# One slot in halves instead of two: the start of an up projection behind a row chain

## The chip, the core and the metric

The kernel runs on one core of a Trainium2 chip. The time is device microseconds of one execution, and the figure that stands for a kernel is the median of its runs. TensorE (PE) does the matmuls and transposes, with weight loads (PEld) that overlap them; VectorE (DVE) and ScalarE (ACT) do the elementwise work and read PE's results from PSUM banks; SyncE (SP) issues the DMAs.

## The reference

One layer of a decoder trunk over 512 positions of 1024 channels: a mixer sub-layer with four branches, then a squared-ReLU MLP, each between two RMS norms and a residual add. Only the seam between the two matters here:

```
mix = merged @ w_out
h   = x + rms_norm(mix, norm_mix_post)
u   = rms_norm(h, norm_mlp_pre)
hid = square(relu(u @ w_up))            # 1024 -> 4096
m   = hid @ w_down                      # 4096 -> 1024
out = h + rms_norm(m, norm_mlp_post)
```

All is float32 in and out.

## The kernel before, in words

Each float32 operand of a matmul is split into a high part (a rounded copy, ACT, L167) and a low part (what is left, DVE, L168), and a product is three matmuls: high by high, low by high, high by low (`mm3`, L237 to L240). Weights come as "units" of 128 x 1024 in the order in which they are used; `unit()` hands out the next one and has those a few ahead loaded (SP) and split.

The 512 positions are four rows of 128 positions, t = 0 to 3 (first to fourth row). Up to the output projection the row is on the partitions: `out_mm(t)` (L867) makes a row's second half of `mix` in a bank `e1[t]`. The first half, `e0`, is made earlier. Then `chain(t)` (L881) runs: ACT squares the bank and sums it, DVE finishes the mean (L847), multiplies by the gain (L884), ACT takes a square root (L855), three small DVE instructions make the reciprocal root (L859 to L861), and two DVE operations over 1024 columns make the residual row `h1` (L886) and the input `u2` of the MLP (L888). The norm before the MLP is not applied with the row's own root here; one known earlier (`rst4`) stands in. The MLP is a squared ReLU between linear maps and is normed again at the end, so the row's own scale only enters through the small constant of that last norm. `row_eps(t)` (L890) works this out from the sum of squares of `h1`: two ACT squares with a read of the sum each, and seven DVE instructions on one element per partition (L845, L847, L893 to L897). Only the end of the kernel reads its result.

The up projection wants `u2` with channels on the partitions. `trans` (L902) turns a row with eight 128 x 128 transposes on PE, and `put` (L911) splits what lies in the bank into `u2h` (ACT) and `u2l` (DVE), 512 columns at a time. Row 0 is turned after `out_mm(2)`, row 1 within `out_mm(3)` (`mid`, L926), rows 2 and 3 within the up projection (L992).

The up projection has 16 slots of 256 hidden channels; a slot takes two units (h = 0, 1) and 48 matmuls of 512 positions (`up_mm`, L945). The first two slots are done in two halves of 256 positions, since rows 2 and 3 come late: first positions 0 to 255 of slots 0 and 1, one unit of each in turn, with the transposes of row 2 behind the second and those of row 3 behind the third; then positions 256 to 511. `up_out` (L958) squares the ReLU of a slot and splits it for the down projection, seven products in place of eight (`form`, `down_group`). The calls of `row_eps` stand behind all this (L1009), and the pools of the mixer are closed ahead of it (L995), so that the down weights' buffers (`load_ab`, L195) reuse the memory of rows that are done with.

The order on each engine is not the program's order but a planner's: it walks a simulated timeline and takes, on each engine, the earliest instruction in program order that it believes ready. `K(...)` holds marked instructions in program order. On the chip each engine then runs its list in that order.

Of the kernel before, what the change touches and what calls it, by code (L numbers as in the profile page):

```python
# [12 lines left out]
AF = mybir.ActivationFunctionType  # L13
ALU = mybir.AluOpType

P = 128
T = 512
D = 1024
NK = D // P
NT = T // P  # L20
# [17 lines left out]
NG = F // (GF * P)  # L38
# [11 lines left out]
def tile_hybrid_trunk(ctx: ExitStack, tc: tile.TileContext, x0, xT, xn, wts, dn, par, bd, cst, msk, gains, out):  # L50
    nc = tc.nc
    act, dve, pool, pe = nc.scalar, nc.vector, nc.gpsimd, nc.tensor
# [17 lines left out]
    K = tc.keep_in_program_order  # L70
# [31 lines left out]
    ident = cp.tile([P, P], F32, name="ident")  # L102
# [6 lines left out]
    rst4 = cp.tile([P, NT], F32, name="rst4")  # L109
# [56 lines left out]
    def split(hi, lo, src, pin=False):  # L166
        a_ = act.activation(hi, src, AF.Copy)  # L167
        d_ = dve.tensor_tensor(lo, src, hi.bitcast(F32), ALU.subtract)  # L168
        if pin:
            K(a_)  # L170
            K(d_)
# [29 lines left out]
    def form(g, n):  # L201
# [22 lines left out]
        split(hi.rearrange("p (j t) -> p j t", j=2), lo.rearrange("p (j t) -> p j t", j=2), src)  # L224
        return hi, lo

    use = [0]
    ahead = [4]
    WARM = 7

    def unit():
        i = use[0]
        use[0] += 1
        prep(i + ahead[0])
        return Wt.hl.pop(i)
# [179 lines left out]
    for c in range(2):  # L415
        for j in range(SCONV):
            src = cx[:, c, PAD - (SCONV - 1) + j : PAD - (SCONV - 1) + j + T]
# [415 lines left out]

    def sq_only(src, t, j):
        dm = s_tile(src.shape[-1])
        act.activation(dm, src, AF.Square, accum_out=stat[:, t, j : j + 1])

    def sq_sum(src, t, j, prev, col):
        sq_only(src, t, j)
# [27 lines left out]
    def out_mm(t, mid=None):  # L867
        e1[t] = sm_bank()
        for k in range(NK):
            if k == 2 and mid:  # L870
                mid()
            wh, wl = wu[k // 2]
            cs = slice((k % 2) * T, (k % 2) * T + T)
            mm3(e1[t], M(0, k, t), M(1, k, t), wh[:, cs], wl[:, cs], k == 0, k == NK - 1)
# [6 lines left out]
    def chain(t):  # L881
        sq = u2[t]
        v = sq_sum(e1[t], t, 1, stat[:, t, 2:3], 3)
        dve.tensor_tensor(sq[:, T:], e1[t], gbc[0][:, T:], ALU.mult)  # L884
        r = row_rstd(v, t)
        dve.scalar_tensor_tensor(h1[t], sq, r, h1[t], ALU.mult, ALU.add)  # L886
        nc.sync.dma_start(h1d[t * P : t * P + P, :], h1[t])
        dve.scalar_tensor_tensor(sq, h1[t], rst4[:, t : t + 1], gbc[1], ALU.mult, ALU.mult)  # L888

    def row_eps(t):  # L890
        e = sq_sum(h1[t][:, :T], t, 4, None, 6)
# [10 lines left out]
    def trans(t, bank):  # L902
        tbs = []
        for j in range(2):
            tb = bank()
            for kk in range(4):
                K(pe.transpose(tb[:, kk * P : kk * P + P], u2[t][:, (4 * j + kk) * P : (4 * j + kk) * P + P], ident))
            tbs.append(tb.rearrange("p (k t) -> p k t", k=4))
        return tbs

    def put(t, j, tv):  # L911
        if u2h[j] is None:
            u2h[j] = up.tile([P, 4, T], F32R, tag="u", name=nm("u2h"))
            u2l[j] = up.tile([P, 4, T], F32R, tag="u", name=nm("u2l"))
        split(u2h[j][:, :, t * P : t * P + P], u2l[j][:, :, t * P : t * P + P], tv)

    for t in range(NT):
        chain0(t)
    for t in range(3):
        out_mm(t)  # L920
        chain(t)
    tb0 = trans(0, sm_bank)
    for j in range(2):
        put(0, j, tb0[j])
# [4 lines left out]
            put(1, j, tb1[j])  # L929

    out_mm(3, mid)
    chain(3)

    mixps.close()
# [4 lines left out]
    def up_bank():  # L939
        return bp.tile([P, 2, T], F32, tag="ub", name=nm("ub"))  # L940

    def dn_bank():
        return dq.tile([P, 2, T], F32, tag="db", name=nm("db"))

    def up_mm(bk, w, h, a, b):  # L945
        wh, wl = w
        for kk in range(4):
            k = 4 * h + kk
            for c in range(2):
                o = kk * W + c * P  # L950
                mm3(bk[:, c, a:b], wh[:, o : o + P], wl[:, o : o + P],
                    U(u2h, k, a, b), U(u2l, k, a, b), k == 0, k == NK - 1)

    HT = T // 2
    NPAIR = 2 * NG
    hid = {}

    def up_out(pair, bk):  # L958
# [19 lines left out]
            split(hi[:, 3:], lo[:, 3:], s)  # L978
        hid[pair] = (hi, lo)

    bks = [up_bank(), up_bank()]
    us = {}
    ahead[0] = 2
    for h in range(2):
        for s in range(2):
            us[s, h] = unit()
            up_mm(bks[s], us[s, h], h, 0, 256)
            if (s, h) in ((1, 0), (0, 1)):
                t = 2 if h == 0 else 3
                tb = dn_bank()  # L990
                for k in range(NK):
                    pe.transpose(tb[:, k // 4, (k % 4) * P : (k % 4) * P + P], u2[t][:, k * P : k * P + P], ident)  # L992
                for j in range(2):
                    put(t, j, tb[:, j].rearrange("p (k t) -> p k t", k=4))
    mix.close()  # L995
    fa = ctx.enter_context(tc.tile_pool(name="fa", bufs=6, reuse_waits="tile"))
    ma = ctx.enter_context(tc.tile_pool(name="ma", bufs=3, reuse_waits="tile"))
# [3 lines left out]
    xp = ctx.enter_context(tc.tile_pool(name="xp", bufs=2, reuse_waits="tile"))  # L1001
    load_ab(0, 0)
    load_ab(0, 1)
    for s in range(2):
        for h in range(2):
            up_mm(bks[s], us[s, h], h, 256, T)
        up_out(s, bks[s])
    ahead[0] = 4
    for t in range(NT):  # L1009
        row_eps(t)  # L1010

    def up_pair(pair):
        bk = up_bank()
# [159 lines left out]
def _layout(inp):  # L1173
    import numpy as np

    a = {k: np.asarray(v) for k, v in inp.items()}
    f4 = np.float32
    x = a["x"][0]
    xt = x.T.reshape(NK, P, T)
    x0 = np.concatenate([xt[0], a["norm_mix_pre"][0].reshape(NK, P).T], axis=1)  # L1180
    xt = xt[1:]
    xn = x.reshape(NT, P, D)

    wi = a["w_in"][0].reshape(2, 4, P, 26, W)
    wb = a["w_branch"][0].reshape(4, 2, P, 2, T)
    wo = a["w_out"][0].reshape(4, 2, P, 2, T)
    wu = a["w_up"][0].reshape(2, 4, P, 16, W)
    wd = a["w_down"][0].reshape(32, P, D)
    units = []

    def slot(w, s):
        for h in range(2):
            units.append(w[h, :, :, s].transpose(1, 0, 2).reshape(P, D))

    for n in SLOT_ORDER:
        if n == "c_g":
            continue
        if n != "c_i":
            slot(wi, SLOT[n])
            continue  # L1200
        for u in range(4):
            w = wi[u // 2, 2 * (u % 2) : 2 * (u % 2) + 2]
            units.append(np.concatenate([w[:, :, SLOT["c_i"]], w[:, :, SLOT["c_g"]]], axis=2).transpose(1, 0, 2).reshape(P, D))
    units[1], units[2] = units[2], units[1]
    for k in GATE_ORDER:
        for dh in range(2):
            for j in range(2):
                slot(wi, 10 + 4 * k + 2 * dh + j)
            units.append(wb[k, :, :, dh].transpose(1, 0, 2).reshape(P, D))
    for eh in range(2):  # L1210
        for ku in range(4):
            units.append(wo[ku, :, :, eh].transpose(1, 0, 2).reshape(P, D))

    def upg(g):
        n = len(units)
        for s in range(2):
            slot(wu, 2 * g + s)
        if g == 0:
            units[n + 1], units[n + 2] = units[n + 2], units[n + 1]

    upg(0)
    for g in range(1, NG):
        upg(g)
    for j in range(GF):
        units.append(wd[GF * (NG - 1) + j])
    wts = np.stack(units)
    dn = wd.reshape(NG, 2, 2, P, D)[: NG - 1].transpose(0, 2, 3, 1, 4)

    def cols(v):
        return v.reshape(-1, 2, P).transpose(2, 0, 1).reshape(P, -1)  # L1230

    win = np.repeat(np.array(WINS), 64)
    pos = np.arange(1, PAD + 1)
    corr = (win[:, None] / np.minimum(pos[None, :], win[:, None])).astype(f4)
    par = np.concatenate([
        cols(a["lru_conv_w"][0]), cols(a["lru_conv_b"]), cols(a["lru_b_a"]), cols(a["lru_b_x"]),
        cols(a["lru_lambda"]), cols(a["pool_scale"]), cols(a["hgrn_lower_bound"]),
        np.concatenate([a["hgrn_norm"][0], a["hgrn_norm"][0]])[:, None],
        cols(a["sconv_w"][0]),
        cols((1.0 / win).astype(f4)),  # L1240
        corr.reshape(2, P, PAD).transpose(1, 0, 2).reshape(P, 2 * PAD),
        (np.arange(P)[:, None] // 64 == np.arange(2)[None, :]).astype(f4),
    ], axis=1)

    def blocks(w):
        n, b = w.shape[0], w.shape[1]
        o = np.zeros((2, P, P), f4)
        for i in range(n):
            c, r = divmod(i * b, P)
            o[c, r : r + b, r : r + b] = w[i]  # L1250
        return o

    bd = np.concatenate([blocks(a["lru_w_a"][0]), blocks(a["lru_w_x"][0]), blocks(a["pool_w"][0])]).transpose(1, 0, 2)
    s = np.arange(P)[:, None]
    msk = []
    for B in MASKED:
        odd = np.arange(P)[(np.arange(P) // B) % 2 == 1][None, :]
        msk.append(s // B == odd // B - 1)
    msk = np.stack(msk).transpose(1, 0, 2).astype(f4)
    cst = np.eye(P, dtype=f4)[None]  # L1260
    gains = np.concatenate([a["norm_mix_post"], a["norm_mlp_pre"], a["norm_mlp_post"]])
    return [x0, xt, xn, wts, dn, par, bd, cst, msk, gains]
# [21 lines left out]
```

## Time and profile before

| what | value |
|---|---|
| median of 3 runs | 745.53 us (745.18 to 745.75) |
| the profiled execution's own time | 745.06 us |
| its span, first to last instruction | 743.3 us |
| PE busy | 735.2 us (99%), 3458 matmuls and transposes |
| DVE busy | 535.8 us (72%) |
| ACT busy | 314.9 us (42%) |
| granted TensorE clock, mean | 0.999 of full speed |

The span leaves out what lies before the first and behind the last instruction. Busy time of a pipelined PE overlaps itself, so PE's pace is read from start to start of its matmuls. A time in a timeline counts from the start of the span.

### The profile page before, as it was taken

Reading aid. Unit: us, or ns where it says so; the run is one execution under the profiler, and the core shown is the slowest. Engines: PE = TensorE matmul, PEld = TensorE weight load, DVE = VectorE, ACT = ScalarE, POOL = GpSimd, SP = SyncE. Lnnn points to the kernel's source line nnn. Section 1 sums busy time; section 2 is a strip of 40 time slices with the busy share of each in tenths; the row PEclk is TensorE's granted clock in tenths of the full one; section 3 lists DMA queues with packets and bytes.
Section 4 is the critical chain, followed back from the end, with each engine's and each line's share of the span. In section 5 each row is a group of like instructions: output and inputs, shape, how many; then the busy total and the mean of one; then the engine's idle time right before and its main releaser. Section 6 shows DMA issues by size and latency. Waiting matters only on the chain.

```text
span 743.3 us, 8800 instructions
## 1 busy us (share of the span) xinstructions
PE 735.2 (99%) x3458; PEld 616.9 (83%) x3458; DVE 535.8 (72%) x784; ACT 314.9 (42%) x411; POOL 6.4 (1%) x11
## 2 busy tenths in 40 slices
PE   9999999999999999999999999999999999999996
PEld 7888888888888888888888988888888888888885
DVE  6798346559997476654748785788769595976797
ACT  7434222336324322232444566544445362635332
POOL 1100000000000000000000000000000000000000
PEclk9999999999999999999999999999999999999999
DMA  9634333222322253323332704142322415030322
GB/s 327 246 115 142 91 106 88 84 86 85 93 82 82 85 216 100 100 94 114 114 113 86 276 37 172 55 142 86 126 101 90 137 57 169 1 114 28 109 91 113
DMA packets 22761, 84.59 MB, mean 114 GB/s; under 512 B 2624, under 2 KB 3520, under 8 KB 20928
## 3 DMA queue, kind: packets, MB, share of 16 engines
q1 hardware_dynamic: 22288, 83.74, 33.5%
q8 instruction: 27, 0.44, 0.3%
q10 hardware_dynamic: 432, 0.29, 0.1%
q14 instruction: 14, 0.11, 0.1%
HBM read 79.83 MB, written 4.19 MB: 113 GB/s over the span
## 4 chain that ended last, share of the span: by engine, by line
PE 98%; DVE 1%; DMA 0%; issue 0%; ACT 0%; DVEq 0%
PE mm L238 14%; PE mm L239 14%; PE mm L240 14%; PE ub L238 8%; PE ub L240 8%; PE ub L239 8%; PE db L238 6%; PE db L240 6%; PE db L239 6%; PE mm L323 3%; PE sm L240 2%; PE sm L239 2%; PE sm L238 2%; PE sm L606 2%; PE tb L1118 0%; PE tb L1117 0%
## 5 line engine op out<-in xcount | busy, mean ns | idle before, releaser
L167 ACT ACTIVATE whi<-raw 128x1024 fp32r<-128x1024 f32 x98 | 103.8, 1062 | 231.0 <-PE mm L239 105.3
L168 DVE TENSOR_TENSOR wlo<-raw,whi 128x1024 fp32r<-128x1024 f32 x98 | 119.5, 1222 | 77.7 <-ACT whi L167 77.5
L240 PE MATMUL mm<-uh,wlo 128*128 128x512 f32 x336 | 131.0, 390 | 0.0
L239 PE MATMUL mm<-ul,whi 128*128 128x512 f32 x336 | 130.9, 389 | 0.0
L238 PE MATMUL mm<-uh,whi 128*128 128x512 f32 x336 | 130.5, 390 | 0.0
L238 PE MATMUL ub<-u2h,whi 128*128 128x512 f32 (+1 forms) x288 | 105.3, 366 | 0.0
L239 PE MATMUL ub<-u2l,whi 128*128 128x512 f32 (+1 forms) x288 | 105.2, 365 | 0.0
L240 PE MATMUL ub<-u2h,wlo 128*128 128x512 f32 (+1 forms) x288 | 105.2, 365 | 0.0
L238 PE MATMUL db<-fhi,ahi 128*128 128x512 f32 x196 | 76.3, 389 | 0.0
L239 PE MATMUL db<-flo,ahi 128*128 128x512 f32 x196 | 76.3, 389 | 0.0
L240 PE MATMUL db<-fhi,alo 128*128 128x512 f32 x196 | 76.2, 389 | 0.0
L240 PEld LDWEIGHTS mm<-uh,wlo 128*128 128x128 f32 x336 | 63.1, 188 | 13.0
L238 PEld LDWEIGHTS mm<-uh,whi 128*128 128x128 f32 x336 | 63.1, 188 | 13.0
L239 PEld LDWEIGHTS mm<-ul,whi 128*128 128x128 f32 x336 | 63.1, 188 | 12.9
L238 PEld LDWEIGHTS ub<-u2h,whi 128*128 128x128 f32 x288 | 54.2, 189 | 8.9 <-DVE u2l L168 0.3
L240 PEld LDWEIGHTS ub<-u2h,wlo 128*128 128x128 f32 x288 | 54.3, 189 | 8.8
L239 PEld LDWEIGHTS ub<-u2l,whi 128*128 128x128 f32 x288 | 54.3, 189 | 8.7
L167 ACT ACTIVATE fhi<-x 128x1024 fp32r<-128x1024 f32 x28 | 29.7, 1061 | 41.1 <-PE db L240 26.5
L1049 DVE TENSOR_TENSOR rows<-rows,db 128x1024 f32<-128x1024 f32 x24 | 29.2, 1218 | 21.8 <-PE db L240 21.7
L238 PEld LDWEIGHTS db<-fhi,ahi 128*128 128x128 f32 x196 | 36.8, 188 | 7.8 <-DVE macc L1049 0.2
L240 PEld LDWEIGHTS db<-fhi,alo 128*128 128x128 f32 x196 | 36.8, 188 | 7.7
L239 PEld LDWEIGHTS db<-flo,ahi 128*128 128x128 f32 x196 | 36.8, 188 | 7.6
(319 smaller groups left out, 1110.6 us busy)
## 6 DMA issues: line engine op xcount, KB each, us to landing
raw<-in_wts_dram SPq DMA_DIRECT2D x102, 512.0 KB, 3.5
ab<-in_dn_dram SPq DMA_DIRECT2D x14, 1024.0 KB, 4.9
t<-in_xn_dram SPq DMA_DIRECT2D x8, 512.0 KB, 7.4
h1d<-t SPq DMA_DIRECT2D x4, 512.0 KB, 2.6
hr<-h1d SPq DMA_DIRECT2D x2, 1024.0 KB, 6.9
xt<-in_xt_dram SPq DMA_DIRECT2D x7, 256.0 KB, 5.0
out_dram<-mg SPq DMA_DIRECT2D x3, 512.0 KB, 2.6
t<-in_gains_dram SPq DMA_DIRECT2D x2, 512.0 KB, 5.8
```

The lines of the kernel that those rows point to most:

```text
L167: a_ = act.activation(hi, src, AF.Copy)
L168: d_ = dve.tensor_tensor(lo, src, hi.bitcast(F32), ALU.subtract)
L238: pe.matmul(ps, lh, rh, start=first, stop=False)
L239: pe.matmul(ps, lh, rl, start=False, stop=False)
L240: pe.matmul(ps, ll, rh, start=False, stop=last)
L323: pe.matmul(fb[s_][c], fw[pair[s_]][wi][:, o_ : o_ + P], U(us_, k), start=first and k == 0, stop=last and k == NK - 1)
L606: pe.matmul(bk[ct][:, cs].rearrange("s (h n b) -> s h n b", h=2, b=B), kk_[:, ct, cs], qo, start=True, stop=True)
L1049: dve.tensor_tensor(macc[p], macc[p], ps, ALU.add)
```

## The change

Slot 0 alone is done in halves, with its two units one behind the other; slot 1 is done over all 512 positions. Rows 2 and 3 are transposed in halves of four, each into a bank of its own, with the split pinned in program order (`half_trans`, new). The last row's two wide DVE operations are done in two halves of 512 columns, and its `h1` is stored behind them. `row_eps` moves: rows 0 and 1 behind the chain of the next row, row 2 ahead of the chain of row 3, row 3 behind the last transposes, with its squares pinned. The up units are laid out in plain order.

```diff
@@ -224,6 +224,7 @@
         split(hi.rearrange("p (j t) -> p j t", j=2), lo.rearrange("p (j t) -> p j t", j=2), src)
         return hi, lo
 
+    HT = T // 2
     use = [0]
     ahead = [4]
     WARM = 7
@@ -833,7 +834,9 @@
 
     def sq_only(src, t, j):
         dm = s_tile(src.shape[-1])
-        act.activation(dm, src, AF.Square, accum_out=stat[:, t, j : j + 1])
+        a_ = act.activation(dm, src, AF.Square, accum_out=stat[:, t, j : j + 1])
+        if t == NT - 1 and j > 3:
+            K(a_)
 
     def sq_sum(src, t, j, prev, col):
         sq_only(src, t, j)
@@ -883,9 +886,11 @@
         v = sq_sum(e1[t], t, 1, stat[:, t, 2:3], 3)
         dve.tensor_tensor(sq[:, T:], e1[t], gbc[0][:, T:], ALU.mult)
         r = row_rstd(v, t)
-        dve.scalar_tensor_tensor(h1[t], sq, r, h1[t], ALU.mult, ALU.add)
+        for a, b in ((0, T), (T, D)) if t == NT - 1 else ((0, D),):
+            hv = h1[t][:, a:b]
+            dve.scalar_tensor_tensor(hv, sq[:, a:b], r, hv, ALU.mult, ALU.add)
+            dve.scalar_tensor_tensor(sq[:, a:b], hv, rst4[:, t : t + 1], gbc[1][:, a:b], ALU.mult, ALU.mult)
         nc.sync.dma_start(h1d[t * P : t * P + P, :], h1[t])
-        dve.scalar_tensor_tensor(sq, h1[t], rst4[:, t : t + 1], gbc[1], ALU.mult, ALU.mult)
 
     def row_eps(t):
         e = sq_sum(h1[t][:, :T], t, 4, None, 6)
@@ -912,13 +917,15 @@
         if u2h[j] is None:
             u2h[j] = up.tile([P, 4, T], F32R, tag="u", name=nm("u2h"))
             u2l[j] = up.tile([P, 4, T], F32R, tag="u", name=nm("u2l"))
-        split(u2h[j][:, :, t * P : t * P + P], u2l[j][:, :, t * P : t * P + P], tv)
+        split(u2h[j][:, :, t * P : t * P + P], u2l[j][:, :, t * P : t * P + P], tv, t > 1)
 
     for t in range(NT):
         chain0(t)
     for t in range(3):
         out_mm(t)
         chain(t)
+        if t:
+            row_eps(t - 1)
     tb0 = trans(0, sm_bank)
     for j in range(2):
         put(0, j, tb0[j])
@@ -929,6 +936,7 @@
             put(1, j, tb1[j])
 
     out_mm(3, mid)
+    row_eps(2)
     chain(3)
 
     mixps.close()
@@ -942,16 +950,15 @@
     def dn_bank():
         return dq.tile([P, 2, T], F32, tag="db", name=nm("db"))
 
-    def up_mm(bk, w, h, a, b):
+    def up_mm(bk, w, h, a, b, ks=(0, 4)):
         wh, wl = w
-        for kk in range(4):
+        for kk in range(*ks):
             k = 4 * h + kk
             for c in range(2):
                 o = kk * W + c * P
                 mm3(bk[:, c, a:b], wh[:, o : o + P], wl[:, o : o + P],
                     U(u2h, k, a, b), U(u2l, k, a, b), k == 0, k == NK - 1)
 
-    HT = T // 2
     NPAIR = 2 * NG
     hid = {}
 
@@ -978,20 +985,25 @@
             split(hi[:, 3:], lo[:, 3:], s)
         hid[pair] = (hi, lo)
 
+    def half_trans(t, j):
+        tb = dn_bank()
+        for kk in range(4):
+            c = (4 * j + kk) * P
+            pe.transpose(tb[:, 0, kk * P : kk * P + P], u2[t][:, c : c + P], ident)
+        put(t, j, tb[:, 0].rearrange("p (k t) -> p k t", k=4))
+
     bks = [up_bank(), up_bank()]
-    us = {}
     ahead[0] = 2
-    for h in range(2):
-        for s in range(2):
-            us[s, h] = unit()
-            up_mm(bks[s], us[s, h], h, 0, 256)
-            if (s, h) in ((1, 0), (0, 1)):
-                t = 2 if h == 0 else 3
-                tb = dn_bank()
-                for k in range(NK):
-                    pe.transpose(tb[:, k // 4, (k % 4) * P : (k % 4) * P + P], u2[t][:, k * P : k * P + P], ident)
-                for j in range(2):
-                    put(t, j, tb[:, j].rearrange("p (k t) -> p k t", k=4))
+    us = [unit()]
+    up_mm(bks[0], us[0], 0, 0, HT)
+    half_trans(2, 0)
+    half_trans(2, 1)
+    us.append(unit())
+    up_mm(bks[0], us[1], 1, 0, HT, (0, 2))
+    half_trans(3, 0)
+    up_mm(bks[0], us[1], 1, 0, HT, (2, 4))
+    half_trans(3, 1)
+    row_eps(3)
     mix.close()
     fa = ctx.enter_context(tc.tile_pool(name="fa", bufs=6, reuse_waits="tile"))
     ma = ctx.enter_context(tc.tile_pool(name="ma", bufs=3, reuse_waits="tile"))
@@ -1001,13 +1013,13 @@
     xp = ctx.enter_context(tc.tile_pool(name="xp", bufs=2, reuse_waits="tile"))
     load_ab(0, 0)
     load_ab(0, 1)
-    for s in range(2):
-        for h in range(2):
-            up_mm(bks[s], us[s, h], h, 256, T)
-        up_out(s, bks[s])
+    for h in range(2):
+        up_mm(bks[0], us[h], h, HT, T)
+    up_out(0, bks[0])
+    for h in range(2):
+        up_mm(bks[1], unit(), h, 0, T)
+    up_out(1, bks[1])
     ahead[0] = 4
-    for t in range(NT):
-        row_eps(t)
 
     def up_pair(pair):
         bk = up_bank()
@@ -1211,16 +1223,8 @@
         for ku in range(4):
             units.append(wo[ku, :, :, eh].transpose(1, 0, 2).reshape(P, D))
 
-    def upg(g):
-        n = len(units)
-        for s in range(2):
-            slot(wu, 2 * g + s)
-        if g == 0:
-            units[n + 1], units[n + 2] = units[n + 2], units[n + 1]
-
-    upg(0)
-    for g in range(1, NG):
-        upg(g)
+    for s in range(2 * NG):
+        slot(wu, s)
     for j in range(GF):
         units.append(wd[GF * (NG - 1) + j])
     wts = np.stack(units)
```

## Rows read from the trace of the kernel before

**Rows 1.** the page: span, PE's busy row, the chain that ended last.
```profile
span 743.3 us, 8800 instructions
PE 735.2 (99%) x3458; PEld 616.9 (83%) x3458; DVE 535.8 (72%) x784; ACT 314.9 (42%) x411; POOL 6.4 (1%) x11
...
PE 98%; DVE 1%; DMA 0%; issue 0%; ACT 0%; DVEq 0%
```
**Rows 2.** waits of PE: who <- for whom: total us, times, longest us.
```profile
PE sm L294 <- DVE spt L561: 1.1, 1, 1.1
```
**Rows 3.** PE by form, 404 to 428.7: xcount, busy us, mean ns, idle.
```profile
L238 PE MATMUL ub<-u2h,whi 128*128 128x256 f32 x64 | 18.2, 287 | 0.0
...
L992 PE MATMUL db<-ident,t 128*128 128x128 f32 x16 | 2.1, 272 | 0.0
```
**Rows 4.** timeline of PE, 428 to 443: start us, duration us, engine, line, operation.
```profile
428.14 0.28 PE L239 MATMUL ub<-u2l,whi 128*128 128x256 f32 x1
...
428.62 0.28 PE L240 MATMUL ub<-u2h,wlo 128*128 128x256 f32 x1
...
439.64 0.39 PE L238 MATMUL db<-fhi,ahi 128*128 128x512 f32 x1
...
442.82 0.39 PE L240 MATMUL db<-fhi,alo 128*128 128x512 f32 x1
```
**Rows 5.** the same timeline around the transposes of the third row.
```profile
409.74 1.04 PE L992 MATMUL db<-ident,t 128*128 128x128 f32 x8
...
410.73 0.28 PE L239 MATMUL ub<-u2l,whi 128*128 128x256 f32 x1
```
**Rows 6.** timeline of PE and PEld where the up projection starts.
```profile
403.60 0.39 PE L240 MATMUL sm<-sp,ylo 128*128 128x512 f32 x1
...
403.88 0.19 PEld L238 LDWEIGHTS ub<-u2h,whi 128*128 128x128 f32 x1 [0.31 <-DVE u2l L168]
```
**Rows 7.** timeline of DVE ahead of that start.
```profile
393.43 0.15 DVE L847 SCALAR_TENSOR_TENSOR stat<-stat 128x1 f32<-128x1 f32 x1
...
394.16 0.15 DVE L859 RECIPROCAL stat<-rt 128x1 f32<-128x1 f32 x1
394.35 0.22 DVE L860 SCALAR_TENSOR_TENSOR nt<-stat,nh 128x1 f32<-128x1 f32 x1
394.60 0.16 DVE L861 SCALAR_TENSOR_TENSOR stat<-nt,stat 128x1 f32<-128x1 f32 x1
394.80 1.28 DVE L886 SCALAR_TENSOR_TENSOR t<-t,stat,t 128x1024 f32<-128x1024 f32 x1
...
397.58 0.16 DVE L847 SCALAR_TENSOR_TENSOR stat<-stat 128x1 f32<-128x1 f32 x1 [0.18 <-ACT s L836]
...
402.54 1.28 DVE L168 TENSOR_TENSOR u2l<-mm,u2h 128x512 fp32r<-128x512 f32 x2
```
**Rows 8.** timeline of DVE in the fourth row's chain.
```profile
406.16 0.16 DVE L893 TENSOR_TENSOR stat<-stat,rst 128x1 f32<-128x1 f32 x1
406.36 0.16 DVE L894 TENSOR_TENSOR stat<-stat,rst 128x1 f32<-128x1 f32 x1
...
410.09 0.15 DVE L895 TENSOR_TENSOR stat<-stat 128x1 f32<-128x1 f32 x1
...
411.07 0.16 DVE L895 TENSOR_TENSOR stat<-stat 128x1 f32<-128x1 f32 x1
```
**Rows 9.** timeline of ACT in the same chain.
```profile
404.61 0.62 ACT L836 ACTIVATE s<-t 128x512 f32<-128x512 f32 x1
...
406.46 0.19 ACT L855 ACTIVATE rt<-stat 128x1 f32<-128x1 f32 x1
...
410.81 0.60 ACT L167 ACTIVATE u2h<-db 128x512 fp32r<-128x512 f32 x1 [0.53 <-PE db L992]
```
**Rows 10.** SP's queue and ACT: loads and first use of down weights.
```profile
411.56 1.28 SPq L198 DMA_DIRECT2D ab<-in_dn_dram  x3
...
420.30 1.06 ACT L167 ACTIVATE fhi<-ab 128x1024 fp32r<-128x1024 f32 x1 [1.90 <-PE ub L239]
```

## The prediction, written before the changed kernel was run

> **What bounds the kernel now.** I read the page first: PE is busy for 735.2 of 743.3 us, and the chain that ended last runs through PE for 98% of the span [rows 1]. The waits of PE name one wait of 1.1 us, among the warming matmuls at the start [rows 2]; what follows PE's last matmul is not touched by the change. So a microsecond is won here only by giving PE less to stream, and any wait that is added ahead of PE is paid in full. Then I read the timelines around 404 us, where the changed code runs: PE, then DVE and ACT, which feed it. PE starts the up projection at 403.88, and its first weight load has stood 0.31 us until a DVE instruction that wrote u2l was done; by its own pitch PE would have been there at 403.60 + 0.23 = 403.83 [rows 6]. The instruction is the last of the four that split the first two rows, the pair from 402.54 to 403.82 [rows 7]. It reads the bank that the first up matmul overwrites. Its slack is nil: PE already lost about 0.05 us to it. That is the reading on which this forecast turns.
>
> **The change part by part.**
>
> *Fewer, longer matmuls.* Before, both first slots are done in 256-column halves: 64 matmuls on each of three lines, 192 in all [rows 3]. After, slot 0 keeps 96 of them, and slot 1 has 48 of 512 columns in place of 96. One of 256 columns takes (428.62 - 428.14) / 4 = 0.120 us from start to start, one of 512 takes (442.82 - 439.64) / 14 = 0.227 us [rows 4]. So PE saves 96 x 0.120 - 48 x 0.227 = 11.52 - 10.88 = 0.64 us, all on the path.
>
> The Trainium skill ("TensorE: Matmul & The Clock Gate", section "Back-to-back issue gap") gives the isolated gap of a matmul at full clock as N/2.4 + 2.5 ns: 109 ns and 216 ns. By it the saving would be an estimated 48 x 2.5 ns = 0.12 us, and the time 0.5 us above what I forecast. The trace does not agree: the shorter one costs 13 ns more than half of the longer, not 2.5, so the rows' figure stands.
>
> *Transposes.* Sixteen before and sixteen after [rows 3]. Before they stand in two groups of eight, after in one of eight and two of four. From the start of eight to the second matmul behind them are 0.99 us, less one matmul's 0.12 is 0.87, or 0.109 each [rows 5]; a charge for joining a group, if it is in there, is at most 0.1 us. I take nothing for the added group, with 0 to 0.1 as bounds.
>
> *Sums of squares.* Each row's sum issues two ACT squares with their reads and seven one-element DVE instructions (L845, L847, L893 to L897). Before, all four rows' run from 404.6 on [rows 9], behind the start of the up projection. After, rows 0 and 1 come in program order ahead of the splits of the first two rows, and row 2 ahead of the fourth row's chain. DVE stands still only 0.18 us between 393 us and 403.8 [rows 7]. So 14 small instructions join a full queue whose last one holds PE. Their price: thirteen such instructions start between 410.09 and 411.07, 0.08 us apart; one that needs the one before it starts 0.20 us later (406.16, 406.36) [rows 8]. Low end: the chain of a row has gaps of 0.19, 0.25 and 0.20 us between its own dependent instructions [rows 7], each holding one more; in two rows that hides 6, and 8 x 0.08 - 0.18 = 0.5 us is left. High end: 4 x 0.07 (taken just under that 0.08) + 10 x 0.20 - 0.18 = 2.1 us. And nothing at all, if the planner sets the splits ahead of the sums. I take 0.7 us, all 14 at the low pitch giving 0.9 and the low end 0.5, since before the planner did mix such instructions with others. The cover is gone here, so all 0.7 us is PE's.
>
> The gain of the same move: before, the fourth row's square root sat on ACT behind other rows' squares from 404.61 until 406.46 [rows 9]. After, at most row 2's two are in its way. The wait that goes is off the path, since before PE had 72 half matmuls (8.6 us) and eight transposes between its start and the fourth row's transposes.
>
> *The fourth row in halves.* Two DVE operations of 1.28 us become four of 512 columns, 0.64 (half) to 0.69 us each (a 512-column DVE subtract, two of them taking 1.28 overlapped) [rows 7]: 0.0 to 0.2 us more on DVE, while the first half is ready one operation earlier. Is it in time? With a start at 404.6, PE needs 24 x 0.12 + 8 x 0.109 + 12 x 0.12 = 5.2 us before the first half of row 3 is transposed: 409.8. DVE has the splits done at 404.5, seven small instructions for row 2 (0.6), the chain from L847 to its first wide operation (394.80 - 393.43 = 1.4 in the second row [rows 7]) and two half operations (1.3): 407.8. Slack 2.0 us, and at the second half (411.6 against 409.1) 2.5 us.
>
> *The splits of rows 2 and 3.* These are now pinned and go through two banks for four groups of transposes, so the third group waits until the first split has read its bank. That split's DVE part follows the fourth row's chain, if DVE keeps program order: 409.1 + 0.7 = 409.8 against 409.8. Then the second pass over slot 0 wants row 3's first split at 412.1: transposes until 410.2, 0.3 until ACT starts and 0.6 of copy [rows 9], 0.7 of subtract: 411.8. Both are about even; I take 0, bounds 0 and 0.8.
>
> *What else moves.* The last store of h1 is issued earlier. Row 3's squares, pinned behind the splits, end about 413.7; the first loads of the down weights, into memory that these rows give up, were issued on SP at 411.56 and may go 2 us later. What they feed starts on ACT at 420.30 [rows 10] and on PE at 439.64 [rows 4]: 19 us of cover. Slot 0 is finished 6 us earlier, slot 1's weights are wanted 10 us later; both ease ACT and DVE. POOL's queue has nothing here. All at nothing.
>
> *Sum.* -0.64 + 0.7 + 0 = +0.06 us on a span of 743.3. The profiled execution's own time is 745.06, 1.76 beside the span, and the median of the runs is 745.53, 0.47 above it. So 745.1 for an execution like the profiled one, 745.6 as a median.
>
> **The rivals.**
>
> *The gain stays (744.9).* The splits go ahead of the sums, or the planner hoists the eight transposes of row 2 (0.87 us) into the wait. For it: out of rows of equal readiness the planner mixed freely on DVE [rows 8]. Against: DVE is full, and the sums come first in program order. 745.53 - 0.64 = 744.9.
>
> *The waits win (747.7, slower).* DVE keeps program order with each dependent instruction 0.20 us apart. The split ends at 403.82 + 2.1 = 405.9, PE loses 2.1 us there; row 2's seven (1.1), the chain (1.4) and four halves (2.8) end at 411.2; the first split of row 2 at 411.9, while PE stands at the third group of transposes from 411.1: 0.8 more. 745.53 - 0.64 + 2.1 + 0.8 = 747.8, less the 0.05 lost already, 747.7. It is slower by over 0.2% once the waits pass 0.64 + 1.49 = 2.1 us. For it: the full queue. Against: the small pitch in [rows 8].
>
> *The halves don't do what they say.* The planner puts the second DVE half behind something else, or the transposes of row 3 late among the matmuls of the second pass. Since nothing waits for row 3 before 409.8, this costs at most the 0.64 again: 745.5, which can't be told from the forecast.
>
> **How the numbers follow.** Forecast (waits of 0.4 to 1.4 us, 745.2 to 746.3): 0.48, the third rival's 0.02 in it. Gain stays: 0.33. Waits win: 0.13. What the rows don't show, such as another order of the planner farther on, in a kernel whose PE has no gap to give: 0.06, faster or slower alike. What can be told from no change is 0.2%, 1.49 us: 744.04 to 747.02. Faster 0.04, nearly all from the unseen; slower 0.13 and 0.02, so 0.15; the same 0.81. The gain alone can't reach 1.49 us. The range takes the rival at 744.9 with the 0.3 us by which runs lie apart, and the slower one's start: 744.6 to 747.1.
>
> **What would show it.** PE's 256-column matmuls on the three lines fall from 192 to 96. PEld's wait ahead of the first up matmul grows from 0.3 to about 1 us, still released by DVE's u2l, with some of L893 to L897 ahead of it on DVE: if it does not, the term of 0.7 is wrong. The fourth row's root comes 0.5 us or more nearer to its square. No wait over 0.3 us at the transposes of row 3; if PE stands there or at the second pass over slot 0, the cover was too thin. A time below 744 or gaps of PE behind 430 us would make the prediction wrong in kind.

## The result, and the profile after

Forecast was no change, 745.6 us in a range of 744.6 to 747.1. Measured: 751.6 us (751.4 to 754.15, five runs) against 745.18 (744.85 to 745.75, five runs beside them). The ratio is 1.0093, 95% interval 1.0082 to 1.0104: slower by 6.4 us.

The head of the page after, as in [rows 1]; the execution took 751.4 us.

```profile
span 749.6 us, 8710 instructions
PE 736.8 (98%) x3410; PEld 614.8 (82%) x3410; DVE 535.2 (71%) x786; ACT 314.3 (42%) x411; POOL 6.4 (1%) x11
...
PE 94%; DVE 3%; ACT 1%; DMA 1%; issue 1%; DVEq 0%; ACTq 0%
```

The span grew by 6.3 us, and PE has 94% of the chain that ended last where it had 98%. Where the chain leaves PE stands in the waits of PE's weight loads (who <- for whom: total us, times, longest us).

```profile
PEld ub L239 <- DVE stat L848: 2.4, 1, 2.4
PEld db L239 <- ACT macc L1059: 1.8, 1, 1.8
PEld ub L239 <- ACT whi L167: 1.6, 1, 1.6
...
PEld db L239 <- ACT fhi L167: 0.7, 1, 0.7
PEld ub L239 <- ACT u2h L167: 0.5, 1, 0.5
PEld ub L240 <- DVE u2l L168: 0.4, 1, 0.4
PEld ub L241 <- DVE wlo L168: 0.3, 1, 0.3
```

Left out is the 1.1 among the warming matmuls, which was there before [rows 2]. Before, the first up matmul's weight load stood 0.31 [rows 6]; of the rest none was there. The matmuls' own starts give the loss: a start later than the pitch of [rows 4] allows. From here on "lost" means that.

| place (us from the span's start) | what PE stood for | lost |
|---|---|---|
| 406.17, first up matmul | u2l of row 1, DVE | 2.10 |
| 414.16 and 414.88, second pass of slot 0 | u2h, u2l of row 3 | 0.41 + 0.27 |
| 438.03, 438.98, 439.48 | unit 73 (whi), the form behind it (fhi), unit 73 (wlo) | 1.30 + 0.39 + 0.27 |
| 454.08, a down matmul | ACT emptying a bank into macc (L1059) | 1.53 |

These make 6.27. The steps behind each wait, 0.08 to 0.11 too long, add 0.45 beyond those of before, and the last matmul ahead of the up projection starts 0.24 later (403.84, in [rows 6] 403.60). Less the 0.64 saved, and less the 0.05 that PE lost at the first up matmul before, that is 6.27, and the spans differ by 749.6 - 743.3 = 6.3.

PE by form, 404 to 428 us, answers to [rows 3]:

```profile
L239 PE MATMUL ub<-u2h,whi 128*128 128x256 f32 x32 | 9.3, 291 | 2.2 <-DVE stat L848 1.9 <-ACT u2h L167 0.3
...
L992 PE MATMUL db<-ident,t 128*128 128x128 f32 x16 | 2.1, 273 | 0.0
```

32 short matmuls on each line where there were 64, and 16 transposes: the change does what it says on PE. DVE ahead of the first up matmul answers to [rows 7] (start, duration):

```profile
399.24 0.16 DVE L898 TENSOR_TENSOR stat<-stat,rst 128x1 f32<-128x1 f32 x1
...
400.57 1.22 DVE L168 TENSOR_TENSOR wlo<-raw,whi 128x1024 fp32r<-128x1024 f32 x1
...
404.24 1.27 DVE L892 SCALAR_TENSOR_TENSOR t<-t,rst,t 128x1024 f32<-128x1024 f32 x1
405.43 0.68 DVE L168 TENSOR_TENSOR u2l<-mm,u2h 128x512 fp32r<-128x512 f32 x1
406.03 0.14 DVE L848 TENSOR_SCALAR stat<-stat 128x1 f32<-128x1 f32 x1
```

The small instructions are there, as forecast; the wlo of 1.22 us among them was not. The wait is put down to the 0.14 us of L848 that ended last; the instruction which read the bank is the u2l ahead of it, done at 406.11. On ACT (same columns), the units' splits of these stretches:

```profile
399.48 1.06 ACT L167 ACTIVATE whi<-raw 128x1024 fp32r<-128x1024 f32 x1
...
436.94 1.04 ACT L167 ACTIVATE whi<-raw 128x1024 fp32r<-128x1024 f32 x1
437.89 1.04 ACT L167 ACTIVATE fhi<-ab 128x1024 fp32r<-128x1024 f32 x1
...
453.02 1.00 ACT L1059 ACTIVATE macc<-db 128x1024 f32<-128x1024 f32 x1
```

Before, these two whi ran one behind the other, straight behind row 3's last u2h:

```profile
416.40 2.00 ACT L167 ACTIVATE whi<-raw 128x1024 fp32r<-128x1024 f32 x2
```

So unit 72 moved 17 us forward, to 399.48, and unit 73 moved 20 us back, to 436.94. No line of the diff names either. The code has the reason: their splits belong to the few that are marked,

```
LATE = (5, 6, 7, 8, 9, 10, 72, 73)        # L149
split(hi, lo, r, i in LATE)               # L188; with True: K(a_) on ACT, K(d_) on DVE
```

and in the traces here the splits of units 72 and 73 never run ahead of the instruction that the program issued just before them on the same engine, their pin. Before, the program issued unit 72's split just behind `put(3, 1)`, and unit 73's just behind the calls of `row_eps`, whose squares were early. After, `row_eps` is gone from there and 73's split follows `up_out(1)`, which waits for the whole of slot 1; 72's, since the calls of `unit()` moved with the slots, follows the split of unit 71, which had run at 384.8.

The first loads of the down weights went from 411.56 [rows 10] to 415.84, and the first form from 420.30 to 437.89. That is a second possible cause of the late waits.

### The profile page after: what moved, and what is told of

It reads as the page before. It is cut to its first block, busy times and chain, and to the rows that moved or that the text cites. A ratio compares the mean times of both kernels' runs of the same rounds, so it can differ in the third digit from the quotient of the medians.

```text
span 749.6 us, 8710 instructions
## 1 busy us (share of the span) xinstructions
PE 736.8 (98%) x3410; PEld 614.8 (82%) x3410; DVE 535.2 (71%) x786; ACT 314.3 (42%) x411; POOL 6.4 (1%) x11
## 4 chain that ended last, share of the span: by engine, by line
PE 94%; DVE 3%; ACT 1%; DMA 1%; issue 1%; DVEq 0%; ACTq 0%
PE mm L239 14%; PE mm L241 14%; PE mm L240 14%; PE ub L240 7%; PE ub L241 7%; PE ub L239 7%; PE db L239 6%; PE db L241 6%; PE db L240 6%; PE mm L324 3%; PE sm L241 2%; PE sm L239 2%; PE sm L240 2%; PE sm L607 2%; DMA ab<-in_dn_dram 1%
## 5 line engine op out<-in xcount | busy, mean ns | idle before, releaser
L239 PE MATMUL ub<-u2h,whi 128*128 128x512 f32 (+1 forms) x272 | 102.7, 378 | 3.3 <-DVE stat L848 1.9
L240 PE MATMUL ub<-u2l,whi 128*128 128x512 f32 (+1 forms) x272 | 102.5, 377 | 0.1
L241 PE MATMUL ub<-u2h,wlo 128*128 128x512 f32 (+1 forms) x272 | 102.5, 377 | 0.0
L239 PEld LDWEIGHTS ub<-u2h,whi 128*128 128x128 f32 x272 | 51.1, 188 | 13.6 <-DVE stat L848 2.4
L240 PEld LDWEIGHTS ub<-u2l,whi 128*128 128x128 f32 x272 | 51.2, 188 | 9.8 <-DVE u2l L168 0.4
L241 PEld LDWEIGHTS ub<-u2h,wlo 128*128 128x128 f32 x272 | 51.2, 188 | 9.6 <-DVE wlo L168 0.3
```

What stands on the lines that cost most here:

```text
L239: pe.matmul(ps, lh, rh, start=first, stop=False)
L240: pe.matmul(ps, lh, rl, start=False, stop=False)
L241: pe.matmul(ps, ll, rh, start=False, stop=last)
```

## The experiments

Theory A: the late waits (438 and 454 us) come from unit 73's pin, and unit 72's free split adds to the first wait. Rival B: they come from the memory that row 3's late squares hold, through the loads of the down weights. All ratios are against the kernel before, run beside.

**Both pins mended.** `prep(n)` has the program issue all splits below n.

```diff
     us = [unit()]
+    prep(72)
     up_mm(bks[0], us[0], 0, 0, HT)
...
     row_eps(3)
+    prep(74)
     mix.close()
```


> The changed kernel, with the splits of units 72 and 73 asked for right behind the fourth row's sum (unit 71 at the start of the up projection), so that their pins hang on that sum's last instructions, as they did before the change. Theory A (pins): in the changed kernel unit 73's split waited behind the whole output of slot 1, which made the waits of PE at 436 to 440 and 454 us (3.7 us together), and unit 72's split floated into DVE's full queue ahead of the first up matmul (1.15 us). Both go: about 751.5 - 4.8 = 746.7 us, with 0.9 us left at the first up matmul and 0.9 at the fourth row's transposes. Rival B (memory): the late waits come from the loads of the down weights, which were issued 4 us later since the fourth row's squares hold the memory; they stay, and only the 1.15 us goes: 750.4 us.

747.63 us (8 runs), ratio 1.0025 [1.0015, 1.0035]. The waits of PEld:

```profile
PEld ub L239 <- DVE u2l L168: 2.2, 1, 2.2
...
```

The splits ran at 415.45 and 416.39, and nothing is left at 438 or 454, although the down weights were still loaded late, at 415.58: B falls. But PE lost 1.92 at the first up matmul with no wlo in DVE's queue, 0.18 less than in the changed kernel and not the 1.15 less that A expected. So A's second half falls too: unit 72 was not what filled that wait. The waits at row 3 stayed as they were.

**One pin alone.** The kernel before, its calls of `row_eps` a few lines up:

```diff
+    for t in range(NT):
+        row_eps(t)
     mix.close()
...
     for s in range(2):
         for h in range(2):
             up_mm(bks[s], us[s, h], h, 256, T)
         up_out(s, bks[s])
     ahead[0] = 4
-    for t in range(NT):
-        row_eps(t)
```


> The kernel before with the calls for the four sums moved a few lines up, ahead of the outputs of slots 0 and 1. They run when they ran before; the one thing that changes is which instruction unit 73's split is pinned behind. Theory A: 2 to 4 us of waits between 434 and 455 us, none at the first up matmul: 747 to 749 us. Rivals B and C: 745.2 us, no change.

752.44 us (4 runs), 1.0093 [1.0078, 1.0108]: as much as the whole change and more than the 747 to 749 expected, from a move that adds and removes no instruction. The down weights were loaded at 412.74, 7.7 us behind the first up matmul (405.06) as before (411.56 and 403.88), so B has no part in it; unit 72 ran at 417.57. The first fence is ACT, the second the waits of PEld.

```profile
434.60 1.06 ACT L167 ACTIVATE ahi<-s 128x1024 fp32r<-128x1024 f32 x1 [1.40 <-DVE s L975]
435.56 1.04 ACT L167 ACTIVATE whi<-raw 128x1024 fp32r<-128x1024 f32 x1
436.51 1.04 ACT L167 ACTIVATE fhi<-ab 128x1024 fp32r<-128x1024 f32 x1
```

```profile
PEld db L238 <- ACT macc L1047: 2.5, 1, 2.5
PEld ub L238 <- ACT whi L167: 1.5, 1, 1.5
```

Unit 73's split stands behind the last `ahi` of slot 1, as the pin says, and the forms of the first down products behind it. Lost there: 1.28, 0.38 and 0.28. Later forms of the same products, three from 449.53 us on without a gap, stand on ACT ahead of the evacuation into macc (452.39), for which PE loses 2.29. The rest is told by the windows (us; busy of PE, PEld, DVE, ACT, POOL with counts; granted clock, DMA share, GB/s):

```profile
440.00:450.00 10.00, 10.00 (x45) 8.28 (x45) 7.28 (x9) 5.35 (x7) 0.00 (x0) 1.00 0.36 147
450.00:454.00 4.00, 1.87 (x8) 1.24 (x7) 4.00 (x6) 4.00 (x5) 0.00 (x0) 1.00 0.00 0
454.00:458.00 4.00, 4.00 (x12) 3.12 (x11) 4.00 (x5) 3.15 (x4) 0.00 (x0) 0.57 0.27 70
458.00:462.00 4.00, 4.00 (x20) 3.30 (x19) 2.28 (x2) 2.71 (x3) 0.00 (x0) 1.00 0.99 411
```

In the four microseconds behind the longest wait the granted clock is 0.57 of full speed, mostly the lower of its levels, 1.2 GHz. PE there, start and duration:

```profile
453.45 0.50 PE L238 MATMUL db<-fhi,ahi 128*128 128x512 f32 x1 [2.13 <-ACT macc L1047]
...
455.10 0.63 PE L240 MATMUL db<-fhi,alo 128*128 128x512 f32 x1
455.52 0.63 PE L238 MATMUL db<-fhi,ahi 128*128 128x512 f32 x1
```

0.42 us from start to start in place of 0.227, for eight matmuls: 1.6 us more. So the pin costs 4.2 us in waits and 5.8 with the slow stretch. From the first up matmul to the end the profiled executions took 345.5 us, before 339.4: 6.1, the small steps behind each wait in it.

**That pin mended in the changed kernel,** unit 72 left free:

```diff
     us = [unit()]
+    prep(73)
...
     row_eps(3)
+    prep(74)
```


> The changed kernel with unit 73 alone asked for behind the fourth row's sum; unit 72's split still floats. By theory A only the late waits go (2.1 us at 438 to 440, 1.6 at 454): 751.5 - 3.7 = 747.8 us, with 2.1 us left at the first up matmul. If the two pins act together and not singly, the late waits stay in part: 749 us or more.

748.37 us (5 runs), 1.0035 [1.0022, 1.0048]. Unit 72 at 400.34, unit 73 at 416.56; the down weights at 416.7, later than in the changed kernel; no wait behind 416 us. The first wait lost 2.10. Beside the 1.92 with both pins mended, unit 72's early split costs 0.2 on top of the moved sums. The changed kernel's late waits are gone by this one pin.

**The slots and halves alone.** The changed kernel, the sums back behind `up_out(1)`:

```diff
-        if t:
-            row_eps(t - 1)
...
-    row_eps(2)
     chain(3)
...
-    row_eps(3)
...
     ahead[0] = 4
+    for t in range(NT):
+        row_eps(t)
```


> The changed kernel with all four rows' sums traced where they were before, behind the outputs of slots 0 and 1; the slots, the halves and the transposes stay as changed. Theory A: unit 73's pin hangs on the fourth row's sum again, so no wait of PE behind 430 us; unit 72's split still floats ahead of the first up matmul (1.1 us there, no small instructions with it); up to 0.9 us at the fourth row's transposes; 0.64 us saved: 745.2 + 1.1 + 0.9 - 0.6 = 746.6 us. Rival C (the sums alone did it all): 745.2 - 0.6 = 744.6 us.

746.57 us (10 runs), 1.0013 [1.0003, 1.0022]. Unit 73 is pinned as before, 72 is free (399.96). DVE:

```profile
402.13 1.22 DVE L168 TENSOR_TENSOR wlo<-raw,whi 128x1024 fp32r<-128x1024 f32 x1
403.27 1.28 DVE L892 SCALAR_TENSOR_TENSOR t<-t,rst,t 128x1024 f32<-128x1024 f32 x1
```

Here wlo alone makes the first wait, 1.06 lost. The two causes don't add: both, 2.10; sums, 1.92; wlo, 1.06. No late wait. At row 3 PE loses 0.41 and 0.28.

**The slots and halves with both pins mended,** the last kernel and:

```diff
     us = [unit()]
+    prep(72)
...
     half_trans(3, 1)
+    prep(74)
```


> The changed kernel with the sums where they were before and both pins mended (unit 71 asked for at the start of the up projection, units 72 and 73 behind the fourth row's split): what is left of the change is the slots, the halves and the transposes. Theory A: the 1.1 us at the first up matmul of the run with the slots alone goes, 0.8 to 0.9 us stay at the fourth row's transposes and the split behind them, 0.64 us are saved: 745.5 to 745.8 us, level with before. Rival (the halves are no cost once the queue is free): 744.9 us.

746.28 us (11 runs), 1.0012 [1.0003, 1.0021]. The first wait is as before, 0.31 us, and there is no late one. What is left stands at row 3's transposes (L989) and the matmul behind them. The waits of PEld, then DVE:

```profile
PEld db L989 <- DVE u2l L168: 0.5, 1, 0.5
PEld ub L240 <- DVE stat L901: 0.4, 1, 0.4
PEld db L989 <- DVE stat L901: 0.4, 1, 0.4
```

```profile
407.40 1.41 DVE L891 SCALAR_TENSOR_TENSOR t<-t,stat,t 128x512 f32<-128x512 f32 x2
...
408.86 1.41 DVE L892 SCALAR_TENSOR_TENSOR t<-t,rst,t 128x512 f32<-128x512 f32 x2
410.19 0.68 DVE L168 TENSOR_TENSOR u2l<-db,u2h 128x512 fp32r<-128x512 f32 x1
```

0.50 + 0.31 + 0.28 = 1.1 lost against 0.64 saved, and a time above the 745.5 to 745.8 expected: this part of the change doesn't pay for itself. The halves of row 3 are not ready in turn: both of L891 run ahead of both of L892. Row 2's first split follows them, and frees at 410.87 the bank that row 3's first transposes (410.92) take.

**The same with the order written out:** row 3's halves held in turn, its transposes and the matmul behind the first four marked, the sums of rows 0 to 2 held behind row 3's root and that of row 3 behind its last split, row 2's transposes in one bank tile. The two `prep` calls stay. The diff shows the main lines.

```diff
     chain(3)
+    for t in range(3):
+        row_eps(t)
...
+            if a:
+                K(i_)           # the second wide half of the fourth row
...
+            if t == NT - 1:
+                K(i_)           # its transposes
...
+        if pin:
+            K(i_)               # the matmul at kk = 2 of the second unit
```


> The same, and: the sums of rows 0 to 2 pinned behind the fourth row's root on ACT; the two operations on the first half of the fourth row held ahead of those on the second; row 2's transposes in one bank tile, row 3's two groups each held at its place among the matmuls; row 3's sum and units 72 and 73 behind its last split. If the waits at the fourth row were the planner's order, no wait over 0.3 us is left between 400 and 460 us: 744.8 to 745.1 us. If they are the chain's own length: 745.5 us or more.

746.43 us (11 runs), 1.0013 [1.0004, 1.0022]. One wait in place of three:

```profile
PEld ub L239 <- ACT u2h L167: 1.4, 1, 1.4
```

1.34 lost at 412.70. The halves ran in turn, the first ready at 408.16. But squares of rows 0 to 2 now stood on ACT until 409.06, ahead of row 2's first split, and PE still did all 48 short matmuls ahead of row 3's transposes (410.92), so the order wanted was not the one got. It leaves open what the halves are worth in the order that they were meant for.

**The sums alone,** in the kernel before:

```diff
         chain(t)
+        if t:
+            row_eps(t - 1)
...
+    row_eps(2)
     chain(3)
...
+    row_eps(3)
     mix.close()
...
     ahead[0] = 4
-    for t in range(NT):
-        row_eps(t)
```


> The kernel before with only the four rows' sums moved to the places that the change gives them; slots, transposes and halves as before. Theory A: 0.9 us of small DVE instructions ahead of the first up matmul, and unit 73's split behind slot 1's output, with waits of 2 to 4 us between 434 and 455 us: 748 to 750 us. Rival B: the fourth row's squares are not pinned here, the loads are not late, so 0.9 us alone: 746.1 us.

753.95 us (4 runs), 1.0105 [1.009, 1.012], more than the whole change and than the 748 to 750 expected. Lost: 1.92 at the first up matmul; 1.27, 0.39 and 0.28 at 438; 2.43 at 454.58, with eight matmuls 0.42 us apart behind it (1.6). That is 7.9 together. The down weights were loaded early, at 411.4, which speaks against B once more.

**The same with unit 73's split issued early:**

```diff
     row_eps(3)
+    prep(74)
     mix.close()
```

> The kernel before with the sums moved as the change moves them, and unit 73 asked for right behind the fourth row's sum, so that its pin is as before. It prices the move of the sums by itself. By the run with mended pins, where the first up matmul lost 1.9 us (1.05 from small DVE instructions of rows 0 and 1, the rest from row 2's squares on ACT between the two splits of row 1): 745.4 + 1.9 = 747.3 us, no late waits. By the forecast's term of 0.7: 746.1 us.

747.81 us (6 runs), 1.0028 [1.0017, 1.004]. The one new wait is the first, 1.92 lost. So the moved sums cost 1.9 us by themselves. The split that PE waited for, and what ran ahead of it (ACT, then DVE):

```profile
404.31 0.58 ACT L167 ACTIVATE u2h<-mm 128x512 fp32r<-128x512 f32 x1
```

```profile
404.63 0.16 DVE L893 TENSOR_TENSOR stat<-stat,rst 128x1 f32<-128x1 f32 x1
404.92 0.69 DVE L168 TENSOR_TENSOR u2l<-mm,u2h 128x512 fp32r<-128x512 f32 x1
```

The split needs the copy `u2h`, and ACT made that copy late, at 404.31, behind row 2's two squares, which had stood there from 403.08. It ended at 404.89, and the split started 0.03 later, when DVE had been through with the three small instructions ahead of it for 0.13 us. So a sum acts on this wait from two sides: through its seven instructions on DVE and through its two squares on ACT. In two runs the sums were taken apart by rows.

**Rows 0 and 1 alone, and row 2 alone:** the last kernel, with row 2's sum taken back, and with those of rows 0 and 1.

```diff
-    row_eps(2)
     chain(3)
...
+    row_eps(2)
     row_eps(3)
     prep(74)
```

```diff
         chain(t)
-        if t:
-            row_eps(t - 1)
...
+    row_eps(0)
+    row_eps(1)
     row_eps(3)
     prep(74)
```

> The kernel before with the sums of rows 0 and 1 alone moved ahead of the first up matmul, and unit 73's split held early as in the run before. Theory of two prices (14 small DVE instructions push the last splits back by about 1.05 us, and row 2's squares on ACT between the two halves of row 1's split make the rest, 0.85): the two halves of u2h follow each other again, and PE loses 1.0 to 1.1 us at the first up matmul; time 746.6. Rival (the small instructions are the whole price, the squares of row 2 only fill time in which row 1's second half waits anyway): PE loses 1.9 us there as before, 747.5.

> The kernel before with the sum of row 2 alone moved ahead of row 3's chain, and unit 73's split held early. Theory of two prices: without the 14 small instructions the DVE queue stands some 1 us earlier, but row 2's squares and its first small instructions are still next to row 1's splits; PE loses 0.3 to 0.9 us at the first up matmul, 745.9 to 746.5. Rival (the small instructions of rows 0 and 1 are the whole price): PE loses 0.1 us there, as in the kernel before, 745.6.

Rows 0 and 1: 746.74 us (10 runs), 1.0016 [1.0006, 1.0025], 1.10 lost. Row 2: 745.91 us (10 runs), 1.0004 [0.9995, 1.0013], 0.77 lost. The 0.05 that PE lost before is in both. Together 1.87, against 1.92 in one. Both rivals fall: rows 0 and 1 are not the whole price, and row 2 has one of its own. In the first run the two splits of row 1 follow each other, and the delay is made earlier (DVE, then ACT; the last fence is DVE in the kernel before):

```profile
398.70 0.15 DVE L847 SCALAR_TENSOR_TENSOR stat<-stat 128x1 f32<-128x1 f32 x1
...
400.28 0.69 DVE L168 TENSOR_TENSOR u2l<-sm,u2h 128x512 fp32r<-128x512 f32 x1
...
404.57 1.28 DVE L168 TENSOR_TENSOR u2l<-mm,u2h 128x512 fp32r<-128x512 f32 x2
```

```profile
399.66 0.58 ACT L167 ACTIVATE u2h<-sm 128x512 fp32r<-128x512 f32 x1
```

```profile
398.32 0.68 DVE L168 TENSOR_TENSOR u2l<-sm,u2h 128x512 fp32r<-128x512 f32 x1
```

From L847 to row 0's first split are 1.58 us, before 0.74 (397.58 [rows 7] to 398.32). Ahead of that split stand four small instructions of row 1 on DVE and, on ACT, row 1's squares ahead of the copy, which ended at 400.24. In the second run row 2's squares stand on ACT from 402.15, ahead of row 1's copies (ACT, then DVE):

```profile
403.40 1.06 ACT L167 ACTIVATE u2h<-mm 128x512 fp32r<-128x512 f32 x2
```

```profile
403.81 0.16 DVE L893 TENSOR_TENSOR stat<-stat,rst 128x1 f32<-128x1 f32 x1
404.00 0.69 DVE L168 TENSOR_TENSOR u2l<-mm,u2h 128x512 fp32r<-128x512 f32 x1
```

The first of the two copies and the third of row 2's small instructions both ended at 403.97, and the split started at 404.00: too close to tell apart. No run moves the squares without the small instructions, so how the 1.9 us divides between ACT and DVE stays open.

## Why the prediction was wrong, step by step

*The reading of the start* was right. PE's first up matmul waits for DVE's last split of row 1, with no slack: in every kernel what was put ahead of that split came back as PE's wait, and where nothing was (slots and halves, pins mended) the wait was 0.31 us as before.

*Fewer, longer matmuls*, 0.64 saved: right in kind and, as far as the balance above closes (6.27 by its parts, 6.3 by the spans), in size. By the Trainium skill's rule ("TensorE: Matmul & The Clock Gate", "Back-to-back issue gap") the saving is an estimated 0.12, and the balance then would miss by 0.5. The changed kernel's short matmuls again start 0.12 us apart.

*Sums of squares*, 0.7 within 0.5 to 2.1: in the range, but mis-sized; 1.9 alone. Two things were left out. Row 2's sum had no price at this place, since program order has it behind the first rows' splits; it cost 0.77. And the term counts small DVE instructions alone. The squares on ACT, an engine busy for 42% of the span, had no price, yet they held up the copies that DVE's splits need. The 14 of rows 0 and 1 cost 1.10 alone, 0.08 each, which is the pitch of [rows 8]; the trace doesn't show it made that way, since most of it is the one stretch of 1.58 us in place of 0.74.

*Row 3 in halves, "slack 2.0 us", and the splits "about even"*, together 0 with 0.8 as upper bound: 0.7 in the changed kernel, where PE had started 2.1 us late and so had given DVE that much more time, and 1.1 without that gift. Three things stood against it. The first half was to be ready at 407.8; in the changed kernel it was at 409.67 (DVE, L892), since the second half's first operation ran ahead of the first half's second. The rival "the halves don't do what they say" looked to the planner's order for this, though not to that one. With the pins mended and the sums back, the split of row 2 behind the fourth row's chain, "409.8 against 409.8", came at 410.19 to 410.87, and PE waited for its bank. And in the changed kernel all eight transposes of row 3 stand behind the 24 short matmuls of the second unit in place of four between them (PE):

```profile
412.75 0.28 PE L241 MATMUL ub<-u2h,wlo 128*128 128x256 f32 x1
412.87 1.03 PE L992 MATMUL db<-ident,t 128*128 128x128 f32 x8
```

Row 3's input was complete at 410.38 there (DVE, L892), and the banks of its transposes were free by 411.69 (DVE, the last split of row 2), so it is the planner's order that made the second pass wait for its split. I had priced that rival at the 0.64 it would give up; it costs that and more, since the shorter first pass is also less cover.

*"What else moves", "all at nothing"* is the step that failed most. It asked of each moved thing what it issues, which memory it frees and which queue it passes. It did not ask what is pinned to the place that it leaves. Unit 73's split was; it cost 1.30 + 0.39 + 0.27 + 1.53 = 3.5 us in the changed kernel, over half of the loss, and alone 4.2, or 5.8 with the slow stretch behind it. That is shown twice, by moving the pin alone in the kernel before, and by mending it alone in the changed one. That marked instructions keep program order stands in the description of the kernel; the prediction did not ask which are marked and what they follow. The 19 us of cover for the down weights were there: loaded 4 us later, they were in time in the kernels with that pin mended.

*The forecast's own test*, "gaps of PE behind 430 us would make the prediction wrong in kind", is what came. The 0.06 for an unseen order was too small for a kernel with a hand-kept order on every engine.

What stays open: two of the five runs of the changed kernel took 753.6 and 754.15 us at a mean granted clock of 0.995, the others 751.4 to 751.6 at 0.997 to 0.998. A slow stretch behind its wait at 454 us, such as the two kernels above show, would explain that; no trace of such a run was taken. Why PE lost 1.53 there in the changed kernel and 2.3 to 2.4 in those two was not tried either. No version beat the kernel before: the best, 746.28 and 745.91, are above its 745.55 beside them, the second by less than its interval can tell.

## What to carry to other kernels

Before moving a block of instructions in a program with hand-made order constraints, list what is constrained relative to it, not only what it issues: a pin that takes "the instruction before me" as its place moves when that one does. Where PE is busy for 99% and an engine ahead of a PE wait has no slack, price what is added in every queue that feeds that wait, the seemingly idle engine's too, and include what the planner may hoist from behind. And a shorter pass on the busy engine is also less cover for the chain beside it: rework what the chain has to meet before the saving is booked.

## What the runs showed of the hardware

A single wait can cost more than its length. In two kernels PE stood 2.1 us or more for one bank, between stretches where it was fully busy, started again at full pitch, and 0.8 and 1.3 us later fell to the lower level of its clock: 0.57 and 0.59 of full speed granted over 4 us, eight matmuls of 512 columns 0.42 us apart in place of 0.227, 1.6 us on top of the wait. In the profiled execution of the changed kernel the wait at the same place lost 1.53 us, and the matmuls behind it kept 0.23 to 0.24 us; behind its first wait, with 2.10 lost, the short ones kept their 0.12 us. What sets the cases apart was not tried. The first two behind the wait at 454 us:

```profile
454.08 0.50 PE L239 MATMUL db<-fhi,ahi 128*128 128x512 f32 x1 [1.36 <-ACT macc L1059]
454.41 0.40 PE L240 MATMUL db<-flo,ahi 128*128 128x512 f32 x1
```
